# A Mamba-2 group's recurrence: plain 32-bit products against three rounded products of a high and a low part

## The chip, the cores and the metric

One Trainium2 chip, one of its cores. The metric is device time in microseconds (us), the median of several runs of the whole kernel. Everything below happens on one core's five engines: TensorE (PE in the profile, with its weight loads as PEld), VectorE (DVE), ScalarE (ACT), GpSimd (POOL) and SyncE (SP), which issues DMAs.

## What is computed

One layer of a hybrid backbone, 256 context tokens ahead of 256 latent tokens, width 2048. An input projection (2048 to 12352 columns) feeds a bidirectional Mamba-2 group and a gated MLP group; both outputs go through one output projection. The change lies in the Mamba-2 part, cut here to what matters:

```python
# 8 groups g of 4 heads (64 wide), state 128, chunks of 128 tokens; x, B, C after convolution and SiLU
states = einsum('bckgn,bckgr,bckgrp->bcgrpn', Bc, decay_to_end, xdt)   # B^T times the weighted x
h      = h * exp(a_tot) + s                                             # from chunk to chunk
y_off  = einsum('bcqgn,bcgrpn,bcqgr->bcqgrp', Cc, h_starts, exp(acs))   # C times the state
y_diag = einsum('bcgqk,bcgrqk,bckgrp->bcqgrp', CB, Lmat, xdt)           # within a chunk
```

The convolution has five taps; both directions are computed, and the scan of the latent tokens starts from the context's final state of the same direction.

## The kernel before

**Projection.** The inputs and weights of the big products are each split in a high part, rounded to the form `float32r`, and a low part, the difference, also rounded. A product is then three TensorE passes: high·high, high·low, low·high (`mm3`, lines 139 to 143; lines 1108 to 1110 and 1155 to 1157 for the rest). Weights arrive in halves of 128x1024; ScalarE writes the high part (`split_hi`, line 495) and VectorE the low one (`split_lo`, line 501), three halves ahead of use. The xBC part has 32 tiles of 128 channels, in the order x, x, B, C for each of the 8 groups (`_tile_order`). An x or B tile is 512 tokens wide (a C tile 256, and only latent tokens). Seven tiles (0 to 3, 12, 13, 15) are done in the first stage; the other 25 (`REST`) follow in the loop of lines 918 to 934, two halves of eight contraction steps each, in two alternating PSUM buffers (`acp`).

**The recurrence, put between.** The work on a group's tiles is interleaved with the projection of later tiles. Each step is a small function; `later(dt, fn)` puts it on a list with a due time, and `pump(dt)` advances a planned clock `now` and emits all steps that are due, by due time. It is called after every two contraction steps with 1.3 units (0.65 for a C tile), that is, after six matmuls. Once emitted, a step's instructions stand in that place of their engine's queue: `manual_schedule` keeps PE, DVE, ACT and POOL in the order of emission, so that a waiting instruction holds up all that stand behind it on its engine. Times written "at 54.6" below, with the word pump, are values of that clock `now`; values of it are no microseconds.

For a tile i, `conv_tile` (line 547) plans: tap0 on ACT (line 560), which reads the projection's PSUM; four more taps on DVE, eight instructions for a 512-wide tile (line 576); SiLU on ACT (line 579). `plan_tile` (line 877) plans the rest: for the two x tiles four transposes on PE (`ssd_x`, line 695) and a copy on ACT (`ssd_xc`, line 699); after the second x tile `ssd_w`: POOL weights x by the decays (lines 707 and 710), two tiles of context into `xw` and one of latent tokens into `xl`; `ssd_sk` on POOL; for the B tile transposes and a copy to `bk` (`ssd_b`, `ssd_bc`). After the C tile come, in this order:

- `ssd_cb` (line 761, PE) and `ssd_states` (lines 778 and 781, PE): C·B, and the states `psc` (from `bk` and `xw`, 512 columns, two tiles summed) and `psl` (from `bk` and `xl`, 256 columns for each direction)
- `ssd_cbm` (769, 770, DVE), `ssd_mb` (806, POOL)
- `ssd_hc` (788, ACT) copies `psc`; `ssd_hd` (794, POOL) multiplies by the chunk's decay; `ssd_hl` (800, DVE) adds `psl`: that gives the two start states of each direction, `hs`
- `ssd_m` (814, 816, DVE) builds the decay matrix in `E`; `ssd_o` (831, PE): C times `hs`; `ssd_yo` (837, DVE), `ssd_ya` (845, POOL)
- `ssd_yd` (857, PE), `ssd_yc` (864, ACT), `ssd_yt` (871, PE), `ssd_yf` (875, DVE)

For the next group, `plan_d` (line 730, ACT), `ssd_min` (737, DVE) and `ssd_e` (743, ACT, an Exp) prepare the decays; `ssd_min` of the second chunk also calls `row_load`, a DMA that POOL issues (line 677) and that waits for that minimum. All products of the recurrence are plain 32-bit ones: the trace shows each of them as two matmul instructions.

Of the kernel before, what the change touches and what calls it, by code (L numbers as in the profile page):

```python
# [44 lines left out]
def tile_hybrid_ssd_mlp(  # L45
# [19 lines left out]
    nc = tc.nc  # L65
# [96 lines left out]
    zt, e = yseg(5)[:, 0:256], yseg(5)[:, 256:512]  # L162
# [9 lines left out]
    def spt(shape, name):  # L172
        return sps.tile(shape, F32, tag="s", name=name)
# [136 lines left out]
    for k in range(KT):  # L310
# [5 lines left out]
        g = k % 4  # L316
        nc.tensor.matmul(pss[32 * g : 32 * g + 32, :], lhsT=ones[:, 0:32], rhs=sq, start=k < 4, stop=k >= KT - 4)
        if g == 3:
            warm(512)
            if k < 12:  # L320
# [7 lines left out]
                     start=True, stop=True)  # L328
# [141 lines left out]
    cv1 = cvs.enter_context(mkpool(name="cv1", bufs=1))  # L470
# [59 lines left out]
    def later(dt, fn):  # L530
        queue.append((now[0] + dt, seq[0], fn))
        seq[0] += 1
# [12 lines left out]
    done = {}  # L545
# [152 lines left out]
    def ssd_xc(g, xi):  # L698
        nc.scalar.copy(gs_[g]["xk"][:, :, xi * P : (xi + 1) * P], gs_[g]["ptx", xi])

    def ssd_w(g):
        S = gs_[g]
        xk, h4 = S["xk"], slice(4 * g, 4 * g + 4)
        xw = cv1.tile([P, 2, 2, 256], F32, tag="xw", name=f"xw{g}")
        for t in range(2):
            for d in range(2):
                nc.gpsimd.tensor_tensor(hp(xw[:, t, d, :]), hp(xk[:, t, :]), bc(wctx(t, d)[:, h4], 2, 64), op=ALU.mult)
        xl = cv1.tile([P, 2, 256], F32, tag="xl", name=f"xl{g}")
        for d in range(2):
            nc.gpsimd.tensor_tensor(hp(xl[:, d, :]), hp(xk[:, 2 + d, :]), bc(wlt(d)[:, h4], 2, 64), op=ALU.mult)  # L710
        S["xw"], S["xl"] = xw, xl

    def ssd_b(g):
        bt = done[4 * g + 2]
        bk = cv1.tile([P, 4, P], F32, tag="bk", name=f"bk{g}")
        p = spt([P, 4, P], f"ptb{g}")
        for t in range(4):
            nc.tensor.transpose(p[:, t, :], bt[:, t * P : (t + 1) * P], ident)
        S = gs_.setdefault(g, {})
        S["bk"], S["ptb"] = bk, p  # L720

    def ssd_bc(g):
        nc.scalar.copy(gs_[g]["bk"], gs_[g]["ptb"])


    def ssd_d(g, c, h2):
# [46 lines left out]
    def ssd_states(g):  # L773
        S = gs_[g]
        bk, xw, xl = S["bk"], S["xw"], S["xl"]
        psc = spt([P, 2, 256], f"psc{g}")
        for t in range(2):
            nc.tensor.matmul(psc, lhsT=bk[:, t, :], rhs=xw[:, t], start=t == 0, stop=t == 1)  # L778
        psl = spt([P, 2, 256], f"psl{g}")
        for d in range(2):  # L780
            nc.tensor.matmul(psl[:, d, :], lhsT=bk[:, 2 + d, :], rhs=xl[:, d, :], start=True, stop=True)
        S["psc"], S["psl"] = psc, psl


    def ssd_hc(g):
        S = gs_[g]
        S["hs"] = cv1.tile([P, 2, 2, 256], F32, tag="hs", name=f"hs{g}")
        nc.scalar.copy(S["hs"].rearrange("p c d x -> p (c d) x")[:, 0:4:3, :], S["psc"])

    def ssd_hd(g):  # L790
        hs, h4 = gs_[g]["hs"], slice(4 * g, 4 * g + 4)
        for d in range(2):
            c = 1 - d
            nc.gpsimd.tensor_tensor(hp(hs[:, c, d, :]), hp(hs[:, 1 - c, d, :]), bc(eat[:, d, h4], 2, 64), op=ALU.mult)

    def ssd_hl(g):
        S = gs_[g]
        for d in range(2):
            hd = S["hs"][:, 1 - d, d, :]
            nc.vector.tensor_tensor(hd, S["psl"][:, d, :], hd, op=ALU.add)  # L800


    def ssd_mb(g, c):
        S = gs_[g]
        M = cv1.tile([P, 4, P], F32, tag="M", name=f"M{g}{c}")
        nc.gpsimd.tensor_tensor(M, bc(S["cbb"][:, c, :], 1, 4),
                                bc(dtt[:, 3 * c, 32 + 4 * g : 36 + 4 * g], 2, P), op=ALU.mult)
        S["M"] = M

    def ssd_m(g, c):  # L810
        S = gs_[g]
        E, M = S["E"], S["M"]
        for h in range(4):
            nc.vector.scalar_tensor_tensor(M[:, h, :], S["cbf"][:, c, :], dtt[:, 3 * c, 4 * g + h : 4 * g + h + 1],
                                           M[:, h, :], op0=ALU.mult, op1=ALU.add)
        nc.vector.tensor_tensor(E[:, c], M, E[:, c], op=ALU.mult)

    def yg(g, c):
        return y[:, c, g * 256 : (g + 1) * 256]

    def ssd_sk(g):
        for c in range(2):
            nc.gpsimd.tensor_tensor(hp(yg(g, c)), hp(gs_[g]["xk"][:, 2 + c, :]), bc(dsk[:, 4 * g : 4 * g + 4], 2, 64),
                                    op=ALU.mult)

    def ssd_o(g):
        S = gs_[g]
        ct, hs = done[4 * g + 3], S["hs"]
        S["pso"] = [spt([P, 2, 256], f"pso{g}{c}") for c in range(2)]
        for c in range(2):  # L830
            nc.tensor.matmul(S["pso"][c], lhsT=ct[:, c * P : (c + 1) * P], rhs=hs[:, c], start=True, stop=True)  # L831

    def ssd_yo(g, c):
        S = gs_[g]
        h4 = slice(4 * g, 4 * g + 4)
        yo = cv1.tile([P, 2, 256], F32, tag=f"yo{c}", name=f"yo{g}{c}")
        nc.vector.tensor_tensor(yo.rearrange("p d (h q) -> p d h q", h=4),
                                S["pso"][c].rearrange("p d (h q) -> p d h q", h=4),
                                bc(eac[:, c, :, h4], 3, 64), op=ALU.mult)
        S["yo", c] = yo  # L840

    def ssd_ya(g, c):
        yo = gs_[g]["yo", c]
        for d in range(2):
            nc.gpsimd.tensor_tensor(yg(g, c), yg(g, c), yo[:, d, :], op=ALU.add)
# [31 lines left out]
    def plan_tile(i, src, d0=0.0, ds=5.2, tx=7.0, tw=1.5, late=0.0, td=0.0):  # L877

        g, r = divmod(i, 4)
        conv_tile(i, src, d0, ds)  # L880
        if r < 2:
            later(d0 + tx, lambda: ssd_x(g, r))
            later(d0 + tx + 0.7, lambda: ssd_xc(g, r))
        if r == 1:
            later(d0 + tx + tw, lambda: ssd_w(g))
            later(d0 + tx + tw + 3, lambda: ssd_sk(g))
        if r == 2:
            later(d0 + tx, lambda: ssd_b(g))
            later(d0 + tx + 0.7, lambda: ssd_bc(g))
        if r == 3:  # L890
            d0 += late
            for t, fn in [(6, ssd_cb), (6, ssd_states), (6.9, ssd_cbm), (7.6, lambda g: ssd_mb(g, 0)), (8, ssd_hc),
                          (8.7, ssd_hd), (9.4, ssd_hl), (9.5, lambda g: ssd_m(g, 0)), (11.2, lambda g: ssd_mb(g, 1)),
                          (12, ssd_o), (12.2, lambda g: ssd_m(g, 1)), (13.9, lambda g: ssd_yo(g, 0)),
                          (14.5, lambda g: ssd_yo(g, 1)), (14.7, lambda g: ssd_ya(g, 0)), (15.3, lambda g: ssd_ya(g, 1)),
                          (16 + td, ssd_yd), (16.9 + td, ssd_yc),
                          (18.6 + td, ssd_yt), (19.3 + td, ssd_yf)]:
# [191 lines left out]
    for blk in range(16):  # L1089
# [83 lines left out]
    for i in range(8):  # L1173
        tk, b = divmod(i, 4)
# [5 lines left out]
    xf = [load_raw(xtok[tk], f"xf{tk}") for tk in range(2)]  # L1180
# [148 lines left out]
```

## Time and profile before

| | us |
|---|---|
| median of 3 runs | 990.47 (990.31 to 990.49) |
| the profiled execution's own time | 989.67 |
| its span, first to last instruction | 987.9 |
| PE busy | 978.8 |
| DVE busy | 621.4 |
| ACT busy | 495.4 |
| POOL busy | 112.5 |

A row of the timeline gives start, duration, engine, line, operation, output<-input and shape; "x4" means that so many instructions are merged, and square brackets give the idle time ahead and what ended it. Matmuls are pipelined, so that a matmul's duration is its whole latency; its price in a stream is the distance from its start to the next one's. The groups' recurrences lie between 163 and 461 us of the span.

### The profile page before, as it was taken

The numbers are of one execution on the slowest core, as the hardware profiler recorded it, in microseconds if no ns is written. First come the engines' busy times: TensorE is split into PE (matmuls) and PEld (weight loads), VectorE is DVE, ScalarE is ACT, GpSimd is POOL, SyncE is SP. The second block draws the span as 40 slices with busy tenths as digits, with TensorE's granted clock in tenths as the row PEclk, the third lists the DMA queues.
The fourth block names the chain that finished last, engine by engine and source line by source line (L and its number), as shares of the span: only waits on it lengthen the run. The fifth ranks groups of instructions, "written<-read, shape, count | busy, mean of one in ns | idle before, by whom it ended". The sixth has DMA issues, their size and how long they took to land.

```text
span 987.9 us, 13929 instructions
## 1 busy us (share of the span) xinstructions
PE 978.8 (99%) x5502; PEld 792.6 (80%) x5502; DVE 621.4 (63%) x949; ACT 495.4 (50%) x762; POOL 112.5 (11%) x162
## 2 busy tenths in 40 slices
PE   9999999999999999999999999999999999999997
PEld 4688888778887878787888888887888888888885
DVE  4444488868886566756767766767555564445636
ACT  4233358566665554545445343454565563346522
POOL 0000002432453222224000000000000000000000
PEclk9999999999999999999999999999999999999999
DMA  9999844233323424145877768774455446556722
GB/s 372 421 418 418 352 149 166 86 129 128 128 75 139 142 98 145 43 169 206 297 302 284 275 257 296 280 274 170 170 180 203 171 170 213 178 206 228 282 86 85
DMA packets 31985, 207.26 MB, mean 210 GB/s; under 512 B 4128, under 2 KB 4384, under 8 KB 8496
## 3 DMA queue, kind: packets, MB, share of 16 engines
q1 hardware_dynamic: 29232, 192.79, 52.0%
q0 software_dynamic: 2112, 12.65, 3.7%
q8 instruction: 43, 0.70, 0.3%
q10 hardware_dynamic: 576, 0.94, 0.3%
q14 instruction: 22, 0.18, 0.1%
HBM read 204.20 MB, written 2.16 MB: 209 GB/s over the span
## 4 chain that ended last, share of the span: by engine, by line
PE 92%; DMA 4%; ACT 2%; DVE 1%; SPq 0%; issue 0%; ACTq 0%
PE pa L1108 12%; PE pa L1110 12%; PE pa L1109 12%; PE psx L141 9%; PE psx L143 9%; PE psx L142 9%; PE pm L1157 3%; PE pm L1155 3%; PE pm L1156 3%; DMA wst<-in_wst_dram 3%; PE pq L1157 2%; PE pq L1156 2%; PE pq L1155 2%; PE psada L249 2%; PE psc L778 1%; PE pso L831 1%
## 5 line engine op out<-in xcount | busy, mean ns | idle before, releaser
L85 DVE TENSOR_TENSOR lo_w<-w,hi_w 128x1024 fp32r<-128x1024 f32 x173 | 210.7, 1224 | 146.0 <-ACT hi_w L84 145.9
L84 ACT CAST hi_w<-w 128x1024 fp32r<-128x1024 f32 x173 | 182.1, 1053 | 204.5 <-PE pa L1110 129.4
L1108 PE MATMUL pa<-hi_w,hhi 128*128 128x512 f32 x512 | 202.3, 395 | 0.0
L1110 PE MATMUL pa<-hi_w,hlo 128*128 128x512 f32 x512 | 199.5, 390 | 0.0
L1109 PE MATMUL pa<-lo_w,hhi 128*128 128x512 f32 x512 | 199.3, 389 | 0.0
L141 PE MATMUL psx<-hhi,hi_w 128*128 128x512 f32 (+1 forms) x400 | 153.4, 383 | 0.0
L143 PE MATMUL psx<-hhi,lo_w 128*128 128x512 f32 (+1 forms) x400 | 145.9, 365 | 0.0
L142 PE MATMUL psx<-hlo,hi_w 128*128 128x512 f32 (+1 forms) x400 | 145.7, 364 | 0.0
L1108 PEld LDWEIGHTS pa<-hi_w,hhi 128*128 128x128 f32 x512 | 96.2, 188 | 20.5 <-issue 1.6
L1110 PEld LDWEIGHTS pa<-hi_w,hlo 128*128 128x128 f32 x512 | 96.1, 188 | 20.3
L1109 PEld LDWEIGHTS pa<-lo_w,hhi 128*128 128x128 f32 x512 | 96.2, 188 | 19.5 <-issue 0.2
L576 DVE SCALAR_TENSOR_TENSOR xbc<-psx,pc,xbc 128x248 f32<-128x248 f32 (+1 forms) x204 | 83.6, 473 | 34.8 <-ACT xbc L560 33.9
L501 DVE TENSOR_TENSOR lo_w<-w,hi_w 128x1024 fp32r<-128x1024 f32 x61 | 77.1, 1271 | 23.7 <-ACT hi_w L495 23.6
L141 PEld LDWEIGHTS psx<-hhi,hi_w 128*128 128x128 f32 x400 | 75.5, 189 | 13.4 <-issue 2.9
L143 PEld LDWEIGHTS psx<-hhi,lo_w 128*128 128x128 f32 x400 | 75.4, 188 | 12.5
L142 PEld LDWEIGHTS psx<-hlo,hi_w 128*128 128x128 f32 x400 | 75.6, 189 | 12.2 <-issue 1.7
L495 ACT CAST hi_w<-w 128x1024 fp32r<-128x1024 f32 x61 | 63.5, 1044 | 26.0 <-PE psx L142 12.9
L966 DVE SCALAR_TENSOR_TENSOR junk<-gate,cb 128x2048 bf16<-128x2048 f32 x16 | 36.7, 2291 | 24.1 <-DMA gate<-in_wada_dram 24.1
L1155 PE MATMUL pm<-hi_w,hhi 128*128 128x512 f32 x128 | 50.0, 390 | 0.0
L1156 PE MATMUL pm<-lo_w,hhi 128*128 128x512 f32 x128 | 49.9, 390 | 0.0
L1157 PE MATMUL pm<-hi_w,hlo 128*128 128x512 f32 x128 | 49.7, 389 | 0.0
L730 ACT ACTIVATE R<-R,y 128x128 f32<-128x128 f32 x128 | 38.8, 391 | 0.0
(248 smaller groups left out, 1333.6 us busy)
## 6 DMA issues: line engine op xcount, KB each, us to landing
w<-in_wlat_dram SPq DMA_DIRECT2D x64, 1024.0 KB, 4.8
w<-in_wout_dram SPq DMA_DIRECT2D x32, 1024.0 KB, 4.8
ada<-in_wada_dram SPq DMA_DIRECT2D x30, 1024.0 KB, 13.4
w<-in_wxbc_dram SPq DMA_DIRECT2D x25, 1024.0 KB, 4.8
gate<-in_wada_dram SPq DMA_DIRECT2D x16, 1024.0 KB, 5.5
R<-acs POOLq DMA_DIRECT2D x8, 1024.0 KB, 5.2
wst<-in_wst_dram SPq DMA_DIRECT2D x15, 480.0 KB, 14.0
xT<-in_xch_dram SPq DMA_DIRECT2D x4, 1024.0 KB, 8.0
```

Of the source, the lines that this page charges most:

```text
L84: nc.scalar.copy(hi, raw)
L85: nc.vector.tensor_tensor(lo, raw, hi.bitcast(F32), op=ALU.subtract)
L141: nc.tensor.matmul(ps, lhsT=whi, rhs=hhi[k][:, s], start=start, stop=False)
L142: nc.tensor.matmul(ps, lhsT=whi, rhs=hlo[k][:, s], start=False, stop=False)
L143: nc.tensor.matmul(ps, lhsT=wlo, rhs=hhi[k][:, s], start=False, stop=stop)
L576: nc.vector.scalar_tensor_tensor(ao, zi, cw[:, k : k + 1], ao, op0=ALU.mult, op1=ALU.add)
L1108: nc.tensor.matmul(pa[tk], lhsT=hhi[k][:, t], rhs=whi[:, w], start=k == 0, stop=False)
L1109: nc.tensor.matmul(pa[tk], lhsT=hhi[k][:, t], rhs=wlo[:, w], start=False, stop=False)
L1110: nc.tensor.matmul(pa[tk], lhsT=hlo[k][:, t], rhs=whi[:, w], start=False, stop=k == KT - 1)
L1155: nc.tensor.matmul(p, lhsT=yh[:, t], rhs=whi[:, w], start=j == 0, stop=False)
L1156: nc.tensor.matmul(p, lhsT=yh[:, t], rhs=wlo[:, w], start=False, stop=False)
L1157: nc.tensor.matmul(p, lhsT=yl[:, t], rhs=whi[:, w], start=False, stop=hf == 0 and j == 15)
```

## The change

For groups 1 to 7 (group 0 keeps the plain products, with its buffers renamed) the weighted x, B transposed, C and the start states are kept in a high and a low part, and each of their products is three rounded ones. `ssd_cb`, `ssd_yd` and the transposes stay plain.

```diff
+    def ssd_w(g, n):                        # n = 0, 1: context tiles; n = 2: latent
+        ...
+        elif n == 0:
+            S["xw"] = [cv1.tile([P, 2, 2, 256], F32R, tag=f"xw{v}", name=f"xw{v}{g}") for v in range(2)]
+        if g and n == 2:
+            S["xl"] = [cv1.tile([P, 2, 256], F32R, tag=f"yo{v}", name=f"xl{v}{g}") for v in range(2)]
+        ...
+        if g:
+            S["xf"] = xf = cv1.tile([P, 2, 256], F32, tag="xf", name=f"xf{g}{n}")
         for d in range(2):
+            nc.gpsimd.tensor_tensor(hp(xf[:, d, :]), hp(xk[:, 2 + d if n == 2 else n, :]), ...)
+
+    def ssd_ws(g, n):
+        ...
+        hi, lo = S["xl"] if n == 2 else [v[:, n] for v in S["xw"]]
+        nc.scalar.copy(hi, S["xf"])
+        nc.vector.tensor_tensor(lo, S["xf"], hi.bitcast(F32), op=ALU.subtract)

     def ssd_bc(g):
+        nc.scalar.copy(hi, gs_[g]["ptb"])
+        ...
+        nc.vector.tensor_tensor(lo, gs_[g]["ptb"], hi.bitcast(F32), op=ALU.subtract)

     ssd_states:
+        parts = ((0, 0), (0, 1), (1, 0))
         for t in range(2):
+            for n, (a, b) in enumerate(parts):
+                nc.tensor.matmul(psc, lhsT=bk[a][:, t, :], rhs=xw[b][:, t], ...)
         for d in range(2):
+            for n, (a, b) in enumerate(parts):
+                nc.tensor.matmul(psl[:, d, :], lhsT=bk[a][:, 2 + d, :], rhs=xl[b][:, d, :], ...)

+    def ssd_ct(g):
+        hi, lo = S["ct"] = [cv1.tile([P, 256], F32R, tag=f"ct{v}", name=f"ct{v}{g}") for v in range(2)]
+        nc.scalar.copy(hi, ct)
+        nc.vector.tensor_tensor(lo, ct, hi.bitcast(F32), op=ALU.subtract)

     def ssd_hd(g):                          # groups 1 to 7: from POOL to DVE
+        S["hd"] = cv1.tile([P, 2, 256], F32, tag="yo0", name=f"hd{g}")
         for d in range(2):
+            hd = S["hd"][:, 1 - d, :]
+            nc.vector.tensor_tensor(hp(hd), hp(S["psc"][:, d, :]), bc(eat[:, d, h4], 2, 64), op=ALU.mult)
+            nc.vector.tensor_tensor(hd, S["psl"][:, d, :], hd, op=ALU.add)
+        nc.scalar.copy(slots(S, 0, 1), S["hd"])
+        nc.vector.tensor_tensor(slots(S, 1, 0), S["psc"], slots(S, 0, 0).bitcast(F32), op=ALU.subtract)

     def ssd_hl(g):
+        nc.vector.tensor_tensor(slots(S, 1, 1), S["hd"], slots(S, 0, 1).bitcast(F32), op=ALU.subtract)

     ssd_o:
+            for n, (a, b) in enumerate(((0, 0), (0, 1), (1, 0)) if g else ((0, 0),)):
+                nc.tensor.matmul(S["pso"][c], lhsT=ct[a][:, c * P : (c + 1) * P], rhs=hs[b][:, c], ...)

     plan_tile:
-            later(d0 + tx + tw, lambda: ssd_w(g))
-            later(d0 + tx + tw + 3, lambda: ssd_sk(g))
+            for n in range(3):
+                later(d0 + tx + tw + 2.7 * n, lambda n=n: ssd_w(g, n))
+                later(d0 + tx + tw + 2.7 * n + 1.3, lambda n=n: ssd_ws(g, n))
+            later(d0 + tx + tw + 7.5, lambda: ssd_sk(g))
...
-            (8, ssd_hc), (8.7, ssd_hd), (9.4, ssd_hl), (9.5, m(0)), (12, ssd_o), (12.2, m(1)), ...
+            (7.7, ssd_ct), (8, ssd_hc), (8.1, ssd_hd), (10.4, ssd_hl), (10.5, m(0)), (12.4, ssd_o), (12.6, m(1)), ...

-            plan_tile(i, ps, ds=7, tx=11.5 if i == 4 else 9, tw=12, late=10)
+            plan_tile(i, ps, ds=7, tx=11.5 if i == 4 else 9, tw=17 if i == 5 else 12, late=12)
-            plan_tile(i, ps, td=1.3 if i < 12 else 0)
+            plan_tile(i, ps, td=1.3 if i < 12 else 0, tw=6 if i == 17 else 1.5)
```

The start states `hs` are written into the buffers `xw0` and `xw1`, and the latent part of the weighted x into `yo0` and `yo1`; `xf`, the unsplit weighted x, is one buffer that the three steps of `ssd_w` share.

More of the change, by code (lines that the diff above doesn't have):

```diff
@@ L722, in ssd_bc @@
     def ssd_bc(g):
-        nc.scalar.copy(gs_[g]["bk"], gs_[g]["ptb"])
+        hi, lo = (gs_[g]["bk"] + [None])[:2]
+        nc.scalar.copy(hi, gs_[g]["ptb"])
+        if g == 0:
+            return
+        nc.vector.tensor_tensor(lo, gs_[g]["ptb"], hi.bitcast(F32), op=ALU.subtract)
     def ssd_d(g, c, h2):
@@ L776, in ssd_states @@
         psc = spt([P, 2, 256], f"psc{g}")
+        parts = ((0, 0), (0, 1), (1, 0))
+        if g == 0:
+            parts, xw, xl = ((0, 0),), [xw], [xl]
+        e = len(parts) - 1
         for t in range(2):
-            nc.tensor.matmul(psc, lhsT=bk[:, t, :], rhs=xw[:, t], start=t == 0, stop=t == 1)
+            for n, (a, b) in enumerate(parts):
+                nc.tensor.matmul(psc, lhsT=bk[a][:, t, :], rhs=xw[b][:, t], start=t + n == 0, stop=t == 1 and n == e)
         psl = spt([P, 2, 256], f"psl{g}")
@@ L785, in ssd_hc, with slots @@
+    def slots(S, v, n):
+        h = S["hs"][v].rearrange("p c d x -> p (c d) x")
+        return h[:, 0:4:3, :] if n == 0 else h[:, 1:3, :]
     def ssd_hc(g):
         S = gs_[g]
-        S["hs"] = cv1.tile([P, 2, 2, 256], F32, tag="hs", name=f"hs{g}")
-        nc.scalar.copy(S["hs"].rearrange("p c d x -> p (c d) x")[:, 0:4:3, :], S["psc"])
+        S["hs"] = [cv1.tile([P, 2, 2, 256], F32R if g else F32, tag=f"xw{v if g else 1}", name=f"hs{v}{g}")
+                   for v in range(2 if g else 1)]
+        nc.scalar.copy(slots(S, 0, 0), S["psc"])
@@ L891, in plan_tile @@
             d0 += late
[L892 to L895, printed above, removed]
+            for t, fn in [(6, ssd_cb), (6, ssd_states), (6.9, ssd_cbm), (7.6, lambda g: ssd_mb(g, 0)), (7.7, ssd_ct), (8, ssd_hc),
+                          (8.1, ssd_hd), (10.4, ssd_hl), (10.5, lambda g: ssd_m(g, 0)), (11.2, lambda g: ssd_mb(g, 1)),
+                          (12.4, ssd_o), (12.6, lambda g: ssd_m(g, 1)), (14.3, lambda g: ssd_yo(g, 0)),
+                          (14.9, lambda g: ssd_yo(g, 1)), (15, lambda g: ssd_ya(g, 0)), (15.6, lambda g: ssd_ya(g, 1)),
                           (16 + td, ssd_yd), (16.9 + td, ssd_yc),
```

49 lines of the change are left out of this document (31 added, 18 removed).

## The prediction

> **What bounds the kernel now.** I read the page's busy shares first, then what TensorE waited for in the stretch where the recurrences lie (160 to 462 us), then busy time by stretch.
>
> ```profile
> PE 978.8 (99%) x5502; PEld 792.6 (80%) x5502; DVE 621.4 (63%) x949; ACT 495.4 (50%) x762; POOL 112.5 (11%) x162
> ```
> ```profile
> PE ptx L695 <- ACT xbc L579: 0.5, 1, 0.5
> ```
> ```profile
> 190.00:300.00 110.00, 110.00 (x584) 88.60 (x583) 86.11 (x164) 69.84 (x119) 44.12 (x56) 1.00 0.31 112
> ```
>
> TensorE is the bound: busy for all 110 us of that stretch, and in the whole of the recurrences it waited once, 0.5 us. So a matmul removed is time won, and a wait put ahead of a matmul is time lost, in full. VectorE (86.11 of 110 us) is the next to fill up, and the change gives it and ScalarE work. The profiled execution took 989.67 us, 0.80 under the median of 990.47; I sum against it and add the 0.80 at the end.
>
> **What TensorE gains.** Starts in the PE timeline, rounded products first, then group 2's plain ones.
>
> ```profile
> 227.96 0.28 PE L143 MATMUL psx<-hhi,lo_w 128*128 128x256 f32 x1
> 228.08 0.40 PE L141 MATMUL psx<-hhi,hi_w 128*128 128x512 f32 x1
> 228.31 0.40 PE L142 MATMUL psx<-hlo,hi_w 128*128 128x512 f32 x1
> ...
> 235.37 0.60 PE L761 MATMUL pcb<-xbc,xbc 128*128 128x128 f32 x4
> 235.81 1.88 PE L778 MATMUL psc<-xw,bk 128*128 128x512 f32 x4
> 237.53 1.03 PE L781 MATMUL psl<-xl,bk 128*128 128x256 f32 x4
> 238.40 0.60 PE L695 MATMUL ptx<-ident,xbc 128*128 128x128 f32 x4
> ```
>
> Two plain products of 512 columns cost 237.53 - 235.81 = 1.72, one 0.86; three rounded ones 3 x 0.23 = 0.69: 0.17 won. At 256 columns 0.87/2 = 0.435 against 3 x 0.12 = 0.36: 0.075. Seven groups have 28 of the first (`psc`, `pso`) and 14 of the second (`psl`): 28 x 0.17 + 14 x 0.075 = **5.8 us won**.
>
> **What the other engines get.** The rows for it: state step and decay matrix on DVE, POOL's products, then POOL, ACT, DVE and PE around group 1's states.
>
> ```profile
> 203.75 0.99 DVE L800 TENSOR_TENSOR hs<-psl,hs 128x256 f32<-128x256 f32 x2 [0.51 <-POOL hs L794]
> 204.66 1.13 DVE L814 SCALAR_TENSOR_TENSOR M<-cbf,dtt,M 128x128 f32<-128x128 f32 x4
> ```
> ```profile
> 206.66 1.04 POOL L806 TENSOR_TENSOR M<-cbb,dtt 128x512 f32<-128x512 f32 x1 [2.37 <-DVE E L816]
> ```
> ```profile
> 334.05 1.17 POOL L710 TENSOR_TENSOR xl<-xk,ed 128x256 f32<-128x256 f32 x2
> ```
>
> ```profile
> 191.09 3.06 POOL L845 TENSOR_TENSOR y<-y,yo 128x256 f32<-128x256 f32 x4 [2.08 <-DVE yo L837]
> 198.47 0.59 POOL L677 DMA_DIRECT2D R<-acs  x1 [4.33 <-issue]
> ```
> ```profile
> 194.03 0.59 ACT L864 COPY yc<-psy 128x512 f32<-128x512 f32 x1 [0.72 <-POOL y L845]
> 194.64 1.28 ACT L743 ACT_TABLE_LOAD   x1
> 197.98 1.06 ACT L743 ACTIVATE E<-E 128x1024 f32<-128x1024 f32 x1 [2.06 <-DVE E L737]
> 199.06 1.28 ACT L579 ACT_TABLE_LOAD   x1
> 200.36 0.63 ACT L579 ACTIVATE xbc<-xbc 128x512 f32<-128x512 f32 x1
> 200.89 1.03 ACT L495 CAST hi_w<-w 128x1024 fp32r<-128x1024 f32 x1
> ```
> ```profile
> 192.41 3.20 DVE L576 SCALAR_TENSOR_TENSOR xbc<-psx,pc,xbc 128x248 f32<-128x248 f32 x8 [0.81 <-ACT xbc L560]
> 195.53 0.68 DVE L737 TENSOR_TENSOR E<-R 128x512 f32<-128x512 f32 x1
> 196.12 1.22 DVE L501 TENSOR_TENSOR lo_w<-w,hi_w 128x1024 fp32r<-128x1024 f32 x1
> 197.26 0.69 DVE L737 TENSOR_TENSOR E<-R 128x512 f32<-128x512 f32 x1
> ```
> ```profile
> 199.91 0.60 PE L761 MATMUL pcb<-xbc,xbc 128*128 128x128 f32 x4
> ```
>
> Per group, in 128x512 pieces unless said: on DVE three differences in `ssd_ws`, one in `ssd_bc`, half a piece in `ssd_ct`, two in `hd`/`hl`, and in `hd` two products of 256 columns that POOL did; on ACT three copies, half a piece for C, and one for the decayed state. Prices, from group 1 and elsewhere: no row shows a difference of 128x512 written in the rounded form, so its bounds are half a weight split (1.22/2 = 0.61, line 501, the same operation) and the minimum of line 737 (0.69, the same shape); I take 0.65, nearer the former's operation and the latter's size. A copy on ACT is 0.59 (`yc`), a 256-column state step 0.4 (two lie 0.91 apart from their successor), two weightings on POOL 1.2. Neither end is below nothing, since the instructions come on top.
>
> That is 6.5 x 0.65 + 2 x 0.4 = 5.0 us of DVE for a group, 35 us in all, and 4.5 x 0.59 = 2.7 of ACT; POOL loses 1.2. Over the 110 us above, with four groups in it, DVE comes to 106: full, but not over. What decides is the order. Each new piece is a wait in an in-order queue, and the three steps of `ssd_w` share one buffer `xf`, so that POOL's next weighting waits for DVE's last difference, and ACT's next copy for POOL. Following `later` and `pump` through the loop gives the order on every engine; I lay the durations along it, group by group.
>
> **Group 1, states.** With tw 17 and late 12 the states go from pump 53.3 (199.91) one pump of six products (6 x 0.227 = 1.37) later, to 201.28, and behind the transposes of tile 8. The new order on DVE: taps, minimum, first difference, weight split, second minimum, `yf`, second difference. The first difference goes in after 196.2 and moves the second minimum's end from 197.95 to 198.7. POOL's row load waits for that minimum and stands ahead of the second weighting: 198.75 + 0.59 + 1.2 = 200.55. ACT copies it to 201.15, and only behind that stand the table load and tile 8's SiLU: 201.15 + 1.28 + 0.63 = 203.1. The transposes want it at 201.28: **1.8 us** lost. Behind that SiLU wait, on ACT, a weight's high part and then the third copy; on DVE the low part of that weight and then the third difference: 203.1 + 1.03 + 1.2 + 0.65 = 205.95. `psl` asks at 203.1 + 0.44 (transposes, as `pcb`'s four) + 0.44 + 6 x 0.23 = 205.35: **0.6**.
>
> **Group 1, output.** `ssd_o` now needs the last difference, `hl`, and `hl` is emitted behind tile 9's taps:
>
> ```profile
> 207.71 0.78 ACT L560 ACTIVATE xbc<-psx,pc 128x512 f32<-128x512 f32 x1 [2.17 <-PE psx L143]
> ```
>
> From `psl`'s end, t = 0, tile 9 ends two pumps later, 2.75; +0.15 to tap0, 0.78, taps 3.15, split 1.13, difference 0.65: 8.6. TensorE is there after five pumps, 6.83, has one product (0.23) to do without it, and waits **1.6 us**. Now POOL and DVE finish `hs` at 204.7 and tile 9's taps begin only behind its tap0 (208.5), so that nothing is late.
>
> **Group 2.** Rows of now:
>
> ```profile
> 215.31 3.37 POOL L845 TENSOR_TENSOR y<-y,yo 128x256 f32<-128x256 f32 x4 [7.61 <-DVE yo L837]
> 221.24 0.59 POOL L677 DMA_DIRECT2D R<-acs  x1 [2.55 <-issue]
> ```
> ```profile
> 223.35 3.20 DVE L576 SCALAR_TENSOR_TENSOR xbc<-psx,pc,xbc 128x248 f32<-128x248 f32 x8 [1.45 <-ACT xbc L560]
> ```
> ```profile
> 227.91 0.63 ACT L579 ACTIVATE xbc<-xbc 128x512 f32<-128x512 f32 x1
> ```
> ```profile
> 216.17 1.09 PE L857 MATMUL psy<-E,xk 128*64 128x128 f32 x16
> 230.83 0.60 PE L718 MATMUL ptb<-ident,xbc 128*128 128x128 f32 x4
> ```
>
> SiLU of tile 10 is done 2.3 us before the B transposes now. In the new order on ACT it stands behind all three copies. Group 1's `hl` ends at 206.6 + 8.6 = 215.2; then `m0` 1.75 (1.13 and a piece), POOL's next M 1.05, `m1` 1.75, first `yo` 0.6: 220.35, and POOL's four `ya` 3.4: 223.8. Weighting 1.2 and copy 0.6: 225.65. Exp with its table load 228.0, tap0 228.75, taps 232.0, split 233.2, second difference 233.85, third weighting 235.1, its copy 235.7, table load and SiLU 237.6. TensorE leaves group 1's output at 216.4 and has, up to the transposes, seven pumps of 1.37, eight of 6 x 0.12, and 1.8 of the recurrence's small products between (`psy` 1.0, two times four transposes): 233.5. It waits **4.1 us**, 1.3 of them already where tile 14 wants the PSUM buffer that tile 10's taps read until 232.0. Output: `hl` stands behind tile 13's taps (`V taps` between `hd` and `hl` again): **1.6**. Then `yd` waits for `m1`, which is behind `hl`, `m0` (1.13 + 0.69), tile 14's taps and a split: **1.2**.
>
> **Groups 3 and 4.**
>
> ```profile
> 263.99 0.63 ACT L579 ACTIVATE xbc<-xbc 128x512 f32<-128x512 f32 x1 [1.53 <-DVE xbc L576]
> ```
> ```profile
> 266.30 0.60 PE L695 MATMUL ptx<-ident,xbc 128*128 128x128 f32 x4
> ```
> ```profile
> 291.88 4.80 POOL L845 TENSOR_TENSOR y<-y,yo 128x256 f32<-128x256 f32 x2 [1.27 <-DVE yo L837]
> ```
> ```profile
> 298.57 0.42 ACT L579 ACTIVATE xbc<-xbc 128x256 f32<-128x256 f32 x1
> 300.34 0.60 PE L761 MATMUL pcb<-xbc,xbc 128*128 128x128 f32 x4
> ```
>
> Tile 16's SiLU has 1.7 us in hand; the chain difference 0.65, weighting 1.2, copy 0.6 and their split come to 3.7 ahead of it: **2.0**. Group 3's output: `hl` precedes the taps, 4.3 against 7.3: nothing. Group 4 (tw 6) weights only behind `ya` of group 3 and around the row load. From group 3's `psl`: `hl` 4.3, `m0`, M and `m1` 4.55, tile 18's taps 3.2, `yo`, split, `yo` 2.45, `ya` 1.7, weighting, copy and difference 2.45, split and second minimum 1.9, row load 0.6, second weighting, copy and difference 2.5, third weighting and copy 1.9, table load and SiLU of tile 19 1.7, semaphores 0.3: 27.6 us. TensorE is at `pcb` after ten pumps of 1.37, eight of 0.72 and 3.6 of the recurrence: 23.0. SiLU is 1.35 us ahead now; it will be late by **4.6**.
>
> **Groups 5 to 7.** No taps stand between `hd` and `hl` and the weighting lies far ahead; only the B tile's SiLU behind the third copy comes level with TensorE (8.55 against 8.5): 0.2 each, **0.6**.
>
> Waits 1.8 + 0.6 + 1.6 + 4.1 + 1.6 + 1.2 + 2.0 + 4.6 + 0.6 = 18.1; less 5.8 is +12.3: 989.67 + 12.3 + 0.8 = **1002.8 us**. The unknown is the waits' size: one link (a weighting, a copy) more or less is about 1 us at each of five places, so 997 to 1008 for this case alone. If the order left no waits at all, the same new work would hide under TensorE's products and cost nothing. DMAs aren't touched except the row load, whose place in POOL's queue is counted; SP's queue is not passed. Weight splits come late by the same waits, but stand three halves (some 16 us) ahead of use. `psc` and `psl` are read for 2 us longer; the six PSUM buffers come round only at `psy`.
>
> **Rivals.**
>
> *The chains don't bind (faster).* If the three pieces flow as planned, 2.7 units apart, so that no SiLU and no state comes late, only the win is left: 989.67 - 5.8 + 0.8 = 984.7; up to 3.5 us of waits still make it faster. For it: 24 of 110 us of DVE are idle between 190 and 300. Against it: that idle time lies in waits for ACT, where the new pieces wait too. It decides where the SiLU of tiles 8, 10 and 19 comes ahead of its transposes or `pcb`. Chance 0.17.
>
> *Only the places fixed by the order bind*: group 1's states and both outputs behind taps, `yd`: 2.4 + 1.6 + 1.6 + 1.2 = 6.8, so +1.0 and 991.5 (989 to 995). Chance 0.15.
>
> *POOL and DVE hold each other up (slower still).* In the row at 291.88 two POOL additions took 4.80 us while DVE ran minima and weight splits, against four in 3.06 at 191.09 beside taps that read PSUM. The new third weighting starts where DVE goes on to a weight split (groups 4 to 7) or to tile 13's neighbour, tile 12, whose taps read SBUF (group 2). At a split's length, 1.2, for each of five: +6, 1008.8. [...] Chance 0.12.
>
> *The rounded form isn't cheaper here*, so that nothing is won: 1008.6. The rows at 227.96 to 228.31 are the same form and shapes: 0.03.
>
> **How the numbers follow.** The forecast has 0.53. Within 0.2% (about 2 us, what a measurement of this kernel can tell from no change) lies a third of the second rival, 0.05; faster 0.17; slower 0.78. 8 in 10: 988 to 1009, which leaves out most of the first rival and the upper end of the third.
>
> **What would show it.** Right: PE waits for ACT line 579's SiLU ahead of `ptx`, `ptb` and `pcb` in groups 1, 2 and 4, 2 to 5 us each, and for DVE ahead of `pso` in groups 1 and 2; groups 5 to 7 each about 0.8 us shorter than now. Wrong: PE's waits in 160 to 462 us under 5 us in sum, or waits of groups 5 to 7 above 1 us each.

## The result and the profile after

The changed kernel takes **1013.23 us** (median of 6 runs, 1011.85 to 1014.28), the kernel before, run beside it, 990.32 (989.57 to 990.49): the ratio is 1.0233, with an interval of 1.022 to 1.0246. Slower, as forecast, and by the mechanism forecast, but by 22.9 us and not by 12.3; the time lies 4 us above the upper end of the range. Of the runs below, one execution (of run 8, 3463 us, with all matmuls some three times as long from first to last) was disturbed and is left out.

The profiled execution of the changed kernel took 1011.85 us, its span is 1009.8. First the busy shares of its page, then what TensorE waited for between 160 and 490 us (engine, tile and line, whom it waited for: us in total, times, longest), then the stretch from 190 to 300 us (length, busy time of PE, PEld, DVE, ACT and POOL, granted clock, DMA share, GB/s).

```profile
PE 981.3 (97%) x5544; PEld 800.4 (79%) x5544; DVE 659.2 (65%) x1012; ACT 513.1 (51%) x797; POOL 107.5 (11%) x148
```
```profile
PE pcb L780 <- ACT xbc L579: 5.4, 1, 5.4
PE ptx L695 <- ACT xbc L579: 5.1, 3, 2.3
PE ptb L733 <- ACT xbc L579: 4.1, 5, 1.3
PE pso L886 <- DVE hs L854: 2.7, 2, 1.5
PE psx L141 <- DVE xbc L576: 2.3, 1, 2.3
PE psy L913 <- DVE E L870: 0.3, 1, 0.3
```
```profile
190.00:300.00 110.00, 98.77 (x506) 80.56 (x505) 90.21 (x171) 65.76 (x116) 36.45 (x45) 0.97 0.27 96
```

Where one wait of 0.5 us stood before, there are 19.9 us of waits in all, at the places and with the releasers that the prediction named: SiLU (line 579) ahead of `ptx`, `ptb` and `pcb`, the last difference (854) ahead of `pso`, tile 10's taps (576) ahead of tile 14's first product. VectorE is busy for 90 of the 110 us: it isn't full. And a column that the prediction passed over has changed: the granted clock, 1.00 before, is 0.97.

How such a wait comes about can be read off group 1. ScalarE's timeline, then GpSimd's, then TensorE's transposes:

```profile
198.97 1.06 ACT L762 ACTIVATE E<-E 128x1024 f32<-128x1024 f32 x1 [1.20 <-DVE E L756]
201.30 0.62 ACT L725 CAST xw<-xf 128x512 fp32r<-128x512 f32 x1 [1.27 <-POOL xf L717]
201.93 1.28 ACT L579 ACT_TABLE_LOAD   x1
203.23 0.63 ACT L579 ACTIVATE xbc<-xbc 128x512 f32<-128x512 f32 x1
```
```profile
199.46 0.59 POOL L677 DMA_DIRECT2D R<-acs  x1 [3.65 <-issue]
200.07 1.20 POOL L717 TENSOR_TENSOR xf<-xk,ed 128x256 f32<-128x256 f32 x2
```
```profile
203.91 0.66 PE L695 MATMUL ptx<-ident,xbc 128*128 128x128 f32 x4 [2.30 <-ACT xbc L579]
```

The row load waits for the second minimum and holds up the second weighting behind it; the copy waits for the weighting; and the table load and SiLU of tile 8, whose input had been there since tile 8's taps ended at 195.78, stand behind the copy. TensorE idles 2.30 us for an activation that had nothing to wait for but its place in the queue.

The clock, from the stretches of the changed kernel in which it was low and a slice ahead of each (columns as above):

```profile
204.00:205.00 1.00, 1.00 (x9) 1.00 (x10) 0.18 (x1) 1.00 (x2) 1.00 (x2) 1.00 0.95 401
205.00:208.50 3.50, 3.50 (x14) 2.99 (x13) 3.47 (x5) 1.69 (x4) 1.09 (x2) 0.52 0.18 75
...
236.00:239.00 3.00, 3.00 (x8) 2.34 (x7) 3.00 (x5) 0.13 (x1) 1.70 (x3) 0.50 0.45 101
...
318.00:324.00 6.00, 3.18 (x10) 2.70 (x11) 3.28 (x5) 3.56 (x5) 2.16 (x4) 0.50 0.52 175
```

Behind tile 14's wait two products of 512 columns follow each other like this:

```profile
236.02 0.63 PE L142 MATMUL psx<-hlo,hi_w 128*128 128x512 f32 x1
236.44 0.63 PE L143 MATMUL psx<-hhi,lo_w 128*128 128x512 f32 x1
```

0.42 us from start to start, where it is 0.23 otherwise. The low clock lasted 3.41 us from 205.1 and 3.41 from 235.9, behind waits that ended at 203.9 and 235.6, and 6.83 from 317.8, from within the longest wait, which ended at 320.8.

**The sum.** From the same early product of the projection to the same one behind group 7 the kernel before needs 291.46 us and the changed one 313.14: 21.7 of the 21.9 by which the spans differ. Sorted by the distance from each matmul's start to the next one's, less what that distance is in an undisturbed stream: waits +21.4 (a wait costs some 0.16 more than the view shows: the view counts from the modelled end of the matmul ahead, and in a stream the next one starts 0.16 before that end, 0.23 behind a start at a duration of 0.39), matmuls in the low-clock stretches +4.9, delays under 0.25 us each +1.4, the products themselves -6.0.

### The profile page after: what moved, and what is told of

The parts are those of the page before. It is cut to its first block, busy times and chain, and to the rows that moved or that the text cites. A ratio compares the mean times of both kernels' runs of the same rounds, so it can differ in the third digit from the quotient of the medians.

```text
span 1009.8 us, 14092 instructions
## 1 busy us (share of the span) xinstructions
PE 981.3 (97%) x5544; PEld 800.4 (79%) x5544; DVE 659.2 (65%) x1012; ACT 513.1 (51%) x797; POOL 107.5 (11%) x148
## 3 DMA queue, kind: packets, MB, share of 16 engines
HBM read 204.20 MB, written 2.16 MB: 204 GB/s over the span
## 4 chain that ended last, share of the span: by engine, by line
PE 65%; DVE 2%; POOL 1%; ACT 1%; issue 1%; DVEq 0%; ACTq 0%
PE pa L1166 12%; PE pa L1168 11%; PE pa L1167 11%; PE psx L141 3%; PE pm L1215 3%; PE pm L1213 3%; PE pm L1214 3%; PE psx L143 3%; PE psx L142 3%; PE pq L1215 2%; PE pq L1213 2%; PE pq L1214 2%; POOL xf L717 1%; DVE xbc L576 1%; PE psg L1108 1%; PE psc L803 1%
## 5 line engine op out<-in xcount | busy, mean ns | idle before, releaser
L141 PE MATMUL psx<-hhi,hi_w 128*128 128x512 f32 (+1 forms) x400 | 150.5, 376 | 2.3 <-DVE xbc L576 2.3
```

What stands on the lines that cost most here:

```text
L141: nc.tensor.matmul(ps, lhsT=whi, rhs=hhi[k][:, s], start=start, stop=False)
```

## The experiments

**Theory:** the new pieces stand in in-order queues ahead of work for which TensorE waits; neither their sum nor TensorE's products are the trouble; and behind the longest waits the clock is lost too. **Rivals:** the rounded products aren't cheaper here; or the load itself is too much, so that a wait taken away in one place comes back in the next. The kernel before, run beside each group of runs, had medians of 989.7 to 990.7 us.

**1. plain_products**: the new work of the other engines, without TensorE's gain. The high parts are left out of the products.

```diff
-        parts = ((0, 0), (0, 1), (1, 0))
+        parts = ((1, 1),)        # one product of the low parts, read as plain 32-bit; ssd_o likewise
```

> The changed kernel with all its new copies and differences, but each of the recurrence's products of groups 1 to 7 is one plain 32-bit product of the two low parts instead of three rounded products (the output leaves out the rest of each product). Theory of waits: the queues and so TensorE's waits stay as they are, and only the win of the rounded form goes, 28 x 0.17 + 14 x 0.075 = 5.8 us: about 1019 us. Rival, that the rounded products are no cheaper here than the plain ones: no change, 1013 us.

Measured 1021.11 us (ratio 1.0312, 1.0295 to 1.033): 7.9 above the changed kernel. The three rounded products are cheaper than the plain one, and the rival falls. 7.9 is more than the 5.8, with a clock of 0.988 against 0.992, so the size was left to kernels with fewer such losses (7 and, with hardly any, 11).

**2. hl_first**: the last difference ahead of tile 9's taps.

```diff
-                          (8.1, ssd_hd), (10.4, ssd_hl), (10.5, lambda g: ssd_m(g, 0)),
+                          (8.1, ssd_hd), (8.2, ssd_hl), (10.5, lambda g: ssd_m(g, 0)),
```

> The changed kernel with the last difference of the start states (hl) due right behind hd, and so ahead of the next tile's taps on DVE. Theory of waits: TensorE's two waits ahead of pso (2.7 us together) and the one ahead of psy (0.3) go, nothing else moves: 1009.5 to 1010.5 us. Rival, that DVE simply has too much work between 190 and 320 us: the order among its instructions doesn't matter, 1012 to 1014 us.

Measured 1011.7 (1.0219, 1.0203 to 1.0235), 1.5 less than the changed kernel, with intervals that overlap, and above the 1009.5 to 1010.5 expected. Group 1's wait ahead of `pso` went, group 2's stayed (1.1 us; in that group the edit doesn't bring `hl` ahead of tile 13's taps). But the wait at tile 14's start grew:

```profile
PE psx L141 <- DVE xbc L576: 3.5, 1, 3.5
```

2.3 before, 3.5 now. TensorE comes earlier to the next wait, whose releaser is as late as it was. Waits along one late chain don't add: here the first was taken away, and the next took what was won.

**3. three_buffers**: groups 1 to 4 get three buffers for the unsplit weighted x (parts of `y` that aren't in use yet), so that a weighting doesn't wait for the difference before it. Work and order stay.

```diff
-            S["xf"] = xf = cv1.tile([P, 2, 256], F32, tag="xf", name=f"xf{g}{n}")
+            own = {1: (seg(5), seg(6)), 2: (seg(6), col(3)), 3: (col(4), col(5)), 4: (col(5), col(6))}
+            xf = own[g][n - 1] if n and g in own else cv1.tile([P, 2, 256], F32, tag="xf", name=f"xf{g}{n}")
```

> The changed kernel with a buffer of its own for each of the three weighted pieces of groups 1 to 4 (parts of y that are not in use yet), so that POOL's next weighting no longer waits for DVE's last difference; same work, same due times. Theory of waits: the waits ahead of ptb in group 2 (1.4), ptx of tile 16 (2.5), ptb in group 4 (0.9) go and the one ahead of pcb in group 4 falls from 5.4 to about 3; the ones ahead of tile 8's ptx (behind the row load) and of tile 14 stay. 7 us less of waits and up to 2 us less at half clock: 1004 to 1007 us. Rival, too much work on DVE and ACT: 1012 to 1014 us.

Measured 1004.12 (1.0145, 1.013 to 1.016): 9.1 us back with the same instructions in the same order. That speaks against the load. The waits fall to 15.6 us, by 4.3 and not by the 7 expected (group 4's `ptb` still waits 0.7, and group 2's `pcb` now waits 1.4), and only one low-clock stretch of 3.41 is left (clock 0.998). Two stretches are gone although the waits ahead of them, tile 8's and tile 14's, are as long as before (2.25 and 2.28); the section on the prediction says why, and so the 9.1 us aren't the buffers' alone. The largest waits of this kernel:

```profile
PE pcb L791 <- ACT xbc L579: 4.4, 2, 3.0
PE pso L897 <- DVE hs L865: 2.9, 2, 1.8
```

**4. filled_waits**: TensorE multiplies ones into a buffer that is overwritten afterwards, in the four longest waits. Nothing is done earlier; only the clock can gain.

```diff
+    def fill(p, n, count):
+        for _ in range(count):
+            nc.tensor.matmul(p, lhsT=ones, rhs=ones[:, 0:1].to_broadcast([P, n]), start=True, stop=True)
     ssd_x:     fill(p, 512, 2) for tiles 8 and 16      tile 14's start: fill(p, 512, 2)
     ssd_cb:    fill(p, 256, 11) for group 4
```

> The changed kernel with needless matmuls of ones put where TensorE waits longest (two of 512 columns ahead of ptx of tiles 8 and 16 and ahead of tile 14, eleven of 256 ahead of group 4's pcb), each set shorter than its wait, so that nothing is delayed but TensorE isn't idle. Theory of the clock: the three stretches at half the granted clock (3.4, 3.4 and 6.8 us, 4.9 us lost in them) go: about 1008 us. Rival, that the halved clock costs nothing since TensorE waits anyway: 1013 us, or more if the matmuls are in the way.

The same three stretches of the changed kernel, then of this one; the clock is the column behind POOL's busy time:

```profile
200.00:206.00 6.00, 3.70 (x20) 2.86 (x19) 1.87 (x2) 4.70 (x8) 3.57 (x7) 0.93 0.78 322
232.00:240.00 8.00, 5.71 (x24) 4.49 (x22) 7.70 (x15) 4.48 (x7) 2.70 (x4) 0.79 0.35 116
310.00:325.00 15.00, 8.97 (x37) 7.30 (x38) 11.24 (x16) 9.34 (x14) 6.07 (x8) 0.77 0.38 140
```
```profile
200.00:206.00 6.00, 5.47 (x26) 3.64 (x24) 2.14 (x3) 4.78 (x7) 3.31 (x6) 1.00 0.86 321
232.00:240.00 8.00, 4.95 (x18) 2.81 (x17) 8.00 (x16) 4.47 (x7) 3.04 (x4) 1.00 0.36 131
310.00:325.00 15.00, 14.37 (x70) 11.91 (x69) 11.55 (x19) 8.44 (x11) 6.07 (x8) 1.00 0.41 141
```

No low clock is left in these stretches: it does follow from the idle time. The time is 1010.28 (1.0213, 1.0189 to 1.0238), 2.9 us less in the medians and not 4.9, and that size isn't shown: the four runs lie between 1009.05 and 1014.71, the intervals overlap, and the two profiled executions differ by only 0.7. Part of what the low clock costs is hidden: group 2's wait for `ptb`, 1.3 in the changed kernel, is 2.8 here, since TensorE comes to it earlier.

**5. group4_alone**: own buffers and another order for group 4 alone: weightings and copies due 3 units earlier, the third behind the Exp.

```diff
+            own = {4: (col(5), col(6))}
+            tws, tss = ((0, 0.1, 3.4), (3.8, 3.9, 9.2)) if g == 4 else ((0, 2.7, 5.4), (1.3, 4.0, 6.7))
-            plan_tile(i, ps, td=1.3 if i < 12 else 0, tw=6 if i == 17 else 1.5)
+            plan_tile(i, ps, td=1.3 if i < 12 else 0, tw=2.7 if i == 17 else 1.5)
```

> The changed kernel with one thing altered: in group 4 the three weighted pieces have buffers of their own and two of the weightings stand ahead of group 3's ya and of the row load, so that SiLU of tile 19 no longer stands behind the chain. Theory of waits: the waits ahead of group 4's ptb and pcb (0.9 and 5.4 us) go, and with them the third stretch at half clock; those of groups 1 to 3 stay to within 0.2 us each: 6.3 + 1.9 = 8 us less, 1004 to 1007 us. Rival, too much work on DVE and ACT, with the wait only shifted: 1010 us or more.

Measured 1007.05 (1.0175, 1.0161 to 1.0189): 6.2 back. The wait ahead of group 4's `pcb` falls from 5.4 to 1.8, not to nothing; the one ahead of its `ptb` (0.7) and the 6.83 us of low clock go. Against the expectation, the other groups didn't stay as they were: group 2's `ptb` waits 2.9 instead of 1.3, and the low clock stands at other places (3.41 us twice, behind that wait and behind tile 16's; mean clock 0.995). The 6.2 us are more than the 4.4 that went from group 4's waits.

**6. reordered**: run 3's buffers, and an order for all groups: group 1 weights earlier, `hl` comes right behind `hd`, and in groups 5 to 7 the third copy moves half a unit, behind the B tile's SiLU.

```diff
+            tws = {1: (0, 0.1, 2.7), 2: (0, 0.1, 0.2), 3: (0, 0.1, 0.2), 4: (0, 0.1, 3.4)}.get(g, (0, 2.7, 5.4))
+            tss = {1: (3.6, 3.65, 7.2), 2: (1.3, 1.8, 10.3), 3: (1.3, 4.0, 6.7), 4: (3.8, 3.9, 9.2)}.get(g, (1.3, 4.0, 7.2))
-                          (7.7, ssd_ct), (8, ssd_hc), (8.1, ssd_hd), (10.4, ssd_hl), ...
+                          (7.65, ssd_ct), (7.9, ssd_hc), (8, ssd_hd), (8.05, ssd_hl), ...
     and tw=15.3 (from 17) for tile 5, tw=2.7 (from 6) for tile 17
```

> The changed kernel, all of its products, copies and differences, with buffers of their own for the weighted pieces of groups 1 to 4, the weightings ahead of ya and of the row load, the third copy behind the SiLU that TensorE waits for, and the last difference of the states ahead of the next taps. Theory of waits: TensorE waits 0 to 3 us in the recurrences, the clock stays at 1.00 there, and the win of 5.8 us shows: 984 to 987.5 us, ratio to before 0.994 to 0.9975. Rival, that DVE and ACT hold too little for the new work in groups 1 to 4: 992 us or more, whatever the order.

Measured 997.11 (1.0083, 1.0069 to 1.0098): 16 us back, but far from what was expected. All waits ahead of `pso` and in groups 5 to 7 are gone; one has grown. This kernel's waits, with ScalarE's and GpSimd's rows ahead of the longest:

```profile
PE psx L141 <- DVE xbc L576: 5.1, 1, 5.1
PE psy L924 <- DVE E L881: 2.7, 2, 2.0
PE pcb L791 <- ACT xbc L579: 2.3, 1, 2.3
PE ptx L695 <- ACT xbc L579: 0.6, 2, 0.5
```
```profile
225.33 0.62 ACT L736 CAST xw<-xf 128x512 fp32r<-128x512 f32 x1 [5.17 <-POOL xf L728]
...
228.73 0.77 ACT L560 ACTIVATE xbc<-psx,pc 128x512 f32<-128x512 f32 x1
```
```profile
219.45 4.71 POOL L912 TENSOR_TENSOR y<-y,yo 128x256 f32<-128x256 f32 x4 [2.58 <-DVE yo L904]
224.12 1.18 POOL L728 TENSOR_TENSOR xf<-xk,ed 128x256 f32<-128x256 f32 x2
```

Tile 10's tap0 (line 560) stands behind a copy (and behind what follows that copy: a table load of 1.28 us, the Exp of 1.06 and a second copy of 0.60), the copy waits for the first weighting, and that stands in GpSimd's queue behind group 1's four additions, which take 4.71 us here beside a weight split and two minima on VectorE, and 4.70 in the changed kernel beside the same. The time lies in the load rival's range (992 or more), and this is its best case. Runs 8 to 11 decide between it and one more place in a queue.

**7. reordered_plain**: the same kernel with the plain products of run 1 (the high parts left out).

> The reordered kernel with one plain product of the low parts in the place of each three rounded ones (the output leaves out the rest of each product). With TensorE's waits gone the price of the products stands alone. Theory of waits: 5.8 us over the reordered kernel, that is, level with the kernel before to 1.5 us. Rival, that the rounded products are no cheaper: the same time as the reordered kernel.

Measured 1002.69 (1.013, 1.0116 to 1.0143): 5.6 us above run 6, and 13.0 above the kernel before, with which it was expected to be level. The gain has the size of the prediction, with a reservation: this kernel's waits are 8.7 us in sum and run 6's 10.7, so the two differ by more than their products. Runs 10 and 11, with 1.7 and 1.3 us of waits, are the cleaner pair.

**8 and 9. reordered2 and reordered2_again**: group 2's first copies go behind tap0 and the taps, group 4's third one behind SiLU, and the decay matrices come earlier. The second label is one more execution of the same kernel, for its profile.

```diff
-   2: (1.3, 1.8, 10.3) ... 4: (3.8, 3.9, 9.2)
+   2: (2.95, 8.15, 10.3) ... 4: (3.8, 3.9, 11.2)
-   (10.5, m(0)), (11.2, mb(1)), (12.4, ssd_o), (12.6, m(1))
+   (9.9, m(0)), (9.95, mb(1)), (12.4, ssd_o), (11.0, m(1))
```

> All of the change's work and the buffers of the reordered kernel; in group 2 the two context pieces' copies and differences are moved behind tap0 and the taps of tile 10, in group 4 the latent piece's copy and difference behind tile 19's SiLU, and the decay matrices come about 1.5 units earlier. Theory (the order of the in-order queues alone decides): the wait of 5.1 us for tile 10's taps, the 2.0 us ahead of group 2's psy and the 2.3 us ahead of group 4's pcb go, and with them the half-clock stretch of 6.83 us; TensorE waits 1 to 4 us in all, and the time is 986 to 990 us, 0 to 4 us under the kernel before: 989.8 less 5.8 won plus what waits are left. Rival (load: the added work on VectorE, ScalarE and GpSimd is too much for the room, and a wait taken away in one place comes back in the next): 995 us or more, with 8 us or more of waits.

> The same kernel as in the run before, whose profiled execution was disturbed from its first product to its last; this one is for the profile. Its fast runs were 990.5 to 993.6 us, so that of the 5.8 us won some 6 must still be lost. Order theory: waits of TensorE of 5 to 7 us in the recurrences, at places not yet reordered (SiLU tiles or the output step psy), none over 2.5 us. Load theory: waits of 3 us or more again at the places that were reordered (tile 10's taps, psy of group 2, pcb of group 4).

Eleven executions lie between 990.5 and 999.5, with a median of 991.59 (1.0027, 1.0011 to 1.0043): above the 986 to 990 expected, and below the load rival's 995. The second label, 992.04 us, has the waits

```profile
PE ptb L744 <- ACT xbc L579: 2.4, 1, 2.4
PE pcb L791 <- ACT xbc L579: 1.8, 2, 1.5
PE psc L814 <- DVE bk L753: 0.6, 1, 0.6
PE ptx L695 <- ACT xbc L579: 0.5, 1, 0.5
PE psy L924 <- DVE E L881: 0.3, 1, 0.3
```

and one low-clock stretch of 3.41 us behind the first of them (mean clock 0.997). The 5.1 is gone. What is left, 5.6 us in sum, stands elsewhere: ahead of group 3's `ptb` and of group 2's `pcb` and `psc`, and only 0.3 at a place that was reordered, group 4's `pcb`.

**10. reordered3**: three more places. Tile 12's taps fill a hole of VectorE in group 1, tile 13's go behind tile 11's, and group 2's first decay matrix goes ahead of tile 14's taps.

```diff
-    plan_tile(12, zq[0], 70, ds=7, tx=9)
-    plan_tile(13, zq[1], 80, ds=7, tx=12.5)
+    plan_tile(12, zq[0], 50.4, ds=28.1, tx=28.6)
+    plan_tile(13, zq[1], 76.8, ds=10.2, tx=15.7)
+    (8.3 if g == 2 else 9.9, m(0)), (8.35 if g == 2 else 9.95, mb(1)), (11.6 if g == 2 else 11.0, m(1))
```

> As the kernel before it, with three places more put in order: the taps of tile 12 go into a stretch of group 1 where VectorE is idle, those of tile 13 behind the taps of tile 11, and group 2's first decay matrix ahead of tile 14's taps and its second one behind them. Order theory: the waits ahead of group 3's ptb (2.4 us) and group 2's pcb and psc (2.1 us) go, with the half-clock stretch behind the former (1.7 us); of the 6.3 us lost in the recurrences 1 to 2 are left, and the time is 985 to 987.5 us, 2.5 to 5 us under the kernel before. Load rival: waits of the same sum come back elsewhere, 990 us or more.

Measured **986.1 us** (986.02 to 986.37), ratio 0.996, 0.9948 to 0.9973: faster than both kernels. Its page, its waits, its stretch from 190 to 300 us, and the taps in the former hole:

```profile
PE 973.6 (99%) x5544; PEld 797.0 (81%) x5544; DVE 660.8 (67%) x1012; ACT 511.9 (52%) x797; POOL 111.4 (11%) x148
```
```profile
PE ptx L695 <- ACT xbc L579: 0.8, 2, 0.5
PE psy L924 <- DVE E L881: 0.5, 1, 0.5
PE pcb L791 <- ACT xbc L579: 0.4, 1, 0.4
```
```profile
190.00:300.00 110.00, 108.69 (x605) 90.96 (x605) 102.51 (x191) 76.59 (x136) 44.81 (x53) 1.00 0.30 106
```
```profile
199.59 3.53 DVE L576 SCALAR_TENSOR_TENSOR xbc<-y,pc,xbc 128x248 f32<-128x248 f32 x8
```

VectorE does 102.51 us of work in those 110, more than in the changed kernel (90.21), and TensorE waits less: 1.7 us in all the recurrences.

**11. reordered3_plain**: run 10 with the plain products (the high parts left out).

> The same kernel with one plain product of the low parts in place of each three rounded ones (the output leaves out the high parts): all the new work of VectorE, ScalarE and GpSimd, and none of TensorE's gain. If order is all, the new work costs nothing by itself and this is the kernel before plus the 1 to 2 us of waits left: 990 to 992 us, 5.8 above the one with rounded products. If the load costs time in itself, 994 us or more.

Measured 991.97 (1.002, 1.0011 to 1.003): 5.9 above run 10, and only 1.9 above the kernel before, with all the new instructions in it. The load rival, which wanted 994 or more, falls.

## Why the prediction went wrong, point by point

**The gain was right.** "5.8 us won": 5.6 and 5.9 measured (runs 6 and 7, 10 and 11), 6.0 in the sum of distances.

**The mechanism and nearly all places were right.** Forecast and measured waits (by the view): tile 8's `ptx` 1.8 and 2.3; group 1's `psl` 0.6 and none; its `pso` 1.6 and 1.5; `ptb` of group 2 with tile 14's start 4.1 and 3.6; its `pso` 1.6 and 1.2; its `psy` 1.2 and 0.3; tile 16's `ptx` 2.0 and 2.3; group 4's `pcb` 4.6 and 5.4. No row shows the 0.3 for semaphores in group 4's chain by itself: in the changed kernel its links lie 0.01 to 0.08 us apart from the first weighting on, and 0.53 from the second minimum to the row load. That these waits come of the order and of the one shared buffer, and not of the amount of work, runs 3, 5, 6 and 10 show.

**The step that failed is the sum "Waits ... = 18.1; less 5.8 is +12.3"**, which set a wait equal to its idle time and had no term for what follows it. Set against the profiled execution, the forecast was 989.67 + 12.3 = 1002.0 and the measurement 1011.85, 9.9 more: 4.9 from matmuls at the low clock, 1.4 from small delays, 3.3 from waits that were sized too low (21.4 as distances against 18.1), less 0.2 from a somewhat larger gain; 0.5 lies outside these rows. The prediction's row for 190 to 300 us had the clock in it, at 1.00, and a sentence beside it, "a wait put ahead of a matmul is time lost, in full"; it was lost more than in full. Run 4 shows that the low clock comes from the idle time; how much of the 4.9 us comes back without it, it leaves open (2.9 in the medians, 0.7 between the profiled executions).

Idle time alone doesn't say where the clock falls. The low stretches lasted 3.41, 3.41 and 6.83 us; two of the three follow waits of 2.3 us, and tile 16's wait of the same length (2.33) was followed by none.

What tells them apart in the traces is how a wait falls on a grid in steps of 3.413 us, the length of a low stretch. The three low stretches start 30.72 and 81.92 us apart, 9 and 24 times 3.413. Cut into windows on this grid, the timeline has nearly all of tile 8's wait in one of them and tile 16's across two (columns as above, TensorE's busy time behind the length):

```profile
201.72:205.13 3.41, 1.22 (x10) 1.18 (x11) 1.00 (x2) 3.38 (x5) 2.32 (x4) 1.00 0.82 346
276.82:280.23 3.41, 1.86 (x9) 1.21 (x7) 1.70 (x2) 0.42 (x1) 1.18 (x2) 1.00 0.31 91
280.23:283.64 3.41, 2.63 (x14) 2.25 (x15) 2.40 (x3) 2.77 (x5) 2.41 (x3) 1.00 0.51 216
```

TensorE is idle for 2.19 us of the first window, and for 1.55 and 0.78 of the others. The same count over the whole spans of both kernels and of ten runs (their twelve profiles, each with the grid that its own low stretches give) finds 29 full-clock windows ahead of a low one, all with at least 1.96 us of idle time, and 3446 others, none with more than 1.82. In the changed kernel the idle times are 2.19 to 2.36 in the four windows ahead of a low one (one of them at the span's end), and at most 1.55 in the others. So, in these profiles, a wait of 2.3 us cost clock where it lay within one window; in run 3 the grid cut the waits of tiles 8 and 14 so that no window had more than 1.82.

**Groups 4 to 7 were sized too low**, by these rows in the way that the third rival supposed. Group 5, GpSimd's weightings, ScalarE's third copy and SiLU, and TensorE:

```profile
355.84 1.18 POOL L717 TENSOR_TENSOR xf<-xk,ed 128x256 f32<-128x256 f32 x2 [1.46 <-DVE xw L726]
361.10 2.10 POOL L717 TENSOR_TENSOR xf<-xk,ed 128x256 f32<-128x256 f32 x2 [4.07 <-DVE xw L726]
```
```profile
363.23 0.62 ACT L725 CAST xl<-xf 128x512 fp32r<-128x512 f32 x1 [4.15 <-POOL xf L717]
363.75 0.62 ACT L579 ACTIVATE xbc<-xbc 128x512 f32<-128x512 f32 x1
```
```profile
364.43 0.65 PE L733 MATMUL ptb<-ident,xbc 128*128 128x128 f32 x4 [0.69 <-ACT xbc L579]
```

VectorE's weight split beside them:

```profile
360.94 1.22 DVE L501 TENSOR_TENSOR lo_w<-w,hi_w 128x1024 fp32r<-128x1024 f32 x1
```

The third weighting takes 2.10 us where the second took 1.18, beside this split: 0.92 longer; those of groups 4, 6 and 7 take 2.10 too, and group 2's, beside tile 12's taps, 1.53. No run shows a delay of a split's length, 1.2, which the rival added at each of its five places: the changed kernel's rows show 0.9 in four of them and 0.35 in the fifth. The forecast had 1.2 for each weighting, hence "0.2 each" for `ptb` in groups 5 to 7 (its own figures, 8.55 against 8.5, give 0.05), where 0.7 was measured (0.86 as a distance), and another 0.7 in group 4. So its sign for these groups, "about 0.8 us shorter", failed as well: they gained 0.88 each by the products and lost 0.86 at `ptb`. The rival's chance of 0.12 was too low; it should have been part of the forecast, at 0.9 for each of four weightings. No run took the overlap away by itself, so this cause is argued from the rows; run 6 took the copy out of SiLU's way, and TensorE no longer waited ahead of `ptb`.

**What the range missed:** it allowed for one cost beyond the forecast, not for two together.

## What to carry to other kernels

Work added to engines that aren't full can still cost TensorE much or nothing, by its place alone: here the same instructions made 1013 us in one order and with one buffer, and 986 in another and with more buffers. So write down, for each engine, what stands behind each new instruction and who waits for that; and when a kernel with a sound gain comes out slower, reorder before giving it up. Price a wait of some 2 us or more on TensorE above its idle time, since it can cost clock too (here two of 2.3 us and one of 5.4 brought 13.65 us at a clock of 0.50, and the matmuls in them 4.9 us more), and don't add up the gains of single repairs along one late chain: here they showed in full only when the last one was made.

## What was not expected of the hardware

- TensorE's granted clock fell to 0.50 behind two waits of 2.3 us, for 3.41 us each, and from within one of 5.4 for 6.83 (6.83 also with one of 5.1 in run 6). Not every wait of 2.3 us had that, by where it fell on the grid of 3.413 us: between 1.82 and 1.96 us of idle time in one window lies the step in the twelve profiles. The grid lies otherwise against the kernel's start in each profile (its lines at 0.33 us and every 3.413 after that in the changed kernel's, at 2.16 in the kernel before's), which would make executions of one kernel differ (run 8: 990.5 to 999.5 us at mean clocks of 0.999 to 0.993); for these eleven that isn't shown, since none of them has a trace.
- GpSimd's additions stretch by more than one split's length (1.2 us), the prediction's price for a weighting: four 128x256 additions took 3.06 us beside taps that read PSUM (the kernel before, 191.09), 4.71 in run 6 beside a split and two minima, and 7.31 in the same kernel in group 3's output, beside two splits, two differences and two minima on VectorE. The row is from that kernel's GpSimd timeline.

```profile
300.23 7.31 POOL L912 TENSOR_TENSOR y<-y,yo 128x256 f32<-128x256 f32 x4 [4.66 <-DVE yo L904]
```
